# The transposed stream in the stream's own tiles, where the first norm sums; the last strip's token halves end apart; the last scaling fused

## The chip, the core and the metric

The kernel runs on one core of a Trainium2 chip. The metric is the device time of one execution in microseconds (us). The time of the kernel before is the median of three runs. Beside them one execution was profiled; its trace is what the numbers below come from.

## What is computed

A decoder trunk of two layers on 256 tokens of width 2048, all in float32. Shortened from the reference:

```python
def reference(x, p, positions, ...):
    for i in range(2):
        h = rms_norm(x, attn_norm_w[i])
        if i == 0:
            x = x + mixer_a(h, a_w_qkv[i], a_w_o[i])      # stick-breaking attention
        else:                                             # i == 1
            k_blocks, v_blocks = shared_kv_blocks(x, kv_norm_w, b_w_kv, positions)
            x = x + mixer_b(h, b_w_q[0], b_w_o[0], k_blocks, v_blocks, positions)
        x = x + conv_ffn(rms_norm(x, ffn_norm_w[i]), ...)
        gate = sigmoid(rms_norm(x, ple_norm_w[i]) @ ple_w_gate[i])
        x = x + gate * (p[i] @ ple_w_proj[i])
    return rms_norm(x, final_norm_w)

def rms_norm(x, w):
    return x * rsqrt(mean(x * x, axis=-1) + 1e-6) * w
```

The change touches the first rms_norm, in front of the first product with a_w_qkv, and the end of the program: the gate of layer 1, its product, and the last rms_norm.

## The kernel before

**Tiles.** A block is 128 of the 2048 model columns; there are 16. The stream x lives in SBUF as two tiles `x[0]`, `x[1]` of 128 tokens by 2048 columns. Products need the stream transposed, as blocks of 128 columns by 256 tokens; the host hands in such a copy, `xT`, for the first norm and product.

**Split products.** A float32 operand is split into a high part, rounded to the matmul's format, and the low rest. `weights` (lines 201 to 221) loads weights into `raw` over the SP queue (four buffers), copies the high part `whi` on ACT (ScalarE) and subtracts the low part `wlo` on DVE (VectorE); `whi` and `wlo` have four buffers of two blocks each. `split_x` (lines 128 to 138) does the same to a stream block after multiplying it by the norm's gain: `h` has its high half from ACT (L133) and its low half from DVE (L134). The norm's row factor 1/rms is not in h; it is applied to the product.

**Strips.** A product is done in strips of 512 output columns. `strip_t` (lines 237 to 250) makes four transposed outputs, one PSUM bank each, and takes the blocks in pairs: for one output of one pair a group of two matmuls with whi (512 wide) and two with wlo (256 wide). `strip_v` (lines 252 to 264) makes one output per token half, three matmuls of 512 columns per block. `steps` (lines 223 to 235) holds the last `tail` blocks back and goes through them output by output, so that the outputs end one after the other. Five banks, tag "acc", serve these products. The banks of a `strip_t` are emptied by `evac` (lines 266 to 273): ACT copies the correction (L268), DVE adds (L269) and multiplies by the row factor (L273).

**The first strip.** `strip_t(wqkv, 0, h, True, load_x)` (L595) loads its weights two blocks at a time, 512 KB, and calls `load_x` (lines 589 to 593) for every pair: a transfer of 256 KB into a ring tile `xT`, then `split_x`. Behind it `late_loads` (lines 109 to 117) loads constants and the 2 MB of x over ACT's queue, and the first `Norm` squares x strip by strip on ACT (L161), sums along the row, makes 1/rms by logarithm and exponential and one step of refinement (lines 167 to 177), and turns it into a row over all partitions by a matmul with a diagonal (lines 180 to 186).

**The end.** In `ple` of layer 1 the last strip (s = 3) runs the small product first, then the gate's; per token half come the sigmoid on ACT (L562), the product and the addition on DVE (L567, L568), the square (L161), and the multiplication by the last norm's gain (L571). Then the last norm, and lines 617 to 624: the eight pieces of 128x512 are scaled by 1/rms, the first token half on DVE (L621), the second on ACT (L623), and stored over SP's and ACT's queues (L624).

**What sets the order.** The program is written in one order, and a scheduler makes from it one queue of instructions per engine, which the engine runs in that order, waiting on semaphores. The weights' splits get priority (`tc.high_priority(offset=AHEAD)`), so they stand ahead of their place. A transfer waits in its queue until the buffer it writes is free, and the transfers behind it wait with it. In the queues before, two groups of the second strip stand in front of the end of the first one, and the first norm's matmul stands in its middle.

## Time and profile before

| what | value |
|---|---|
| time, median of 3 runs | 2397.92 us (2396.64 to 2398.55) |
| profiled execution | 2399.31 us |
| its span in the trace | 2397.5 us |
| busy: TensorE matmuls / weight loads | 2363.2 / 2003.5 us |
| busy: VectorE / ScalarE | 1561.1 / 1271.8 us |
| moved by DMA | 442.82 MB, 185 GB/s on average |
| chain of work that ended last | TensorE 97% of the span |

A busy figure is the sum over the whole span; what a stage is limited by is read from that stage. The span is 1.8 us shorter than the execution's time. In the rows, PE is TensorE, PEld its weight loads, SPq and ACTq the DMA queues of SP and ACT, and L220 is line 220 of the kernel before. A timeline's row can hold several instructions (x2); then the second number is the time from the first one's start to the last one's end. Matmuls are pipelined, so the rows of one engine overlap.

### The profile page before, as it was taken

To read this page: it belongs to the slowest core of one execution; us is meant where nothing else is said; L and a number is where in the kernel's file an instruction comes from. 1 tells how busy PE (TensorE), PEld (TensorE's weight loads), DVE (VectorE), ACT (ScalarE), POOL (GpSimd) and SP (SyncE) were. 2 spreads that over 40 slices of the span, in tenths; PEclk is the share of its full clock that TensorE was granted. 3 is DMA by queue.
4 is the path that set the end of the run, shared out by engine and by line. 5 is a ranking of instruction groups with operands and counts; after the bars stand their busy time and mean duration, and the time that the engine had idled before them with its cause. 6 is when DMAs were issued, how large, how long until landed. Compare 5 with 4: busy or idle time off the path is not lost.

```text
span 2397.5 us, 31193 instructions
## 1 busy us (share of the span) xinstructions
PE 2363.2 (99%) x12260; PEld 2003.5 (84%) x12260; DVE 1561.1 (65%) x2364; ACT 1271.8 (53%) x1829; POOL 0.2 (0%) x4
## 2 busy tenths in 40 slices
PE   6999999999999999999999999999999999999997
PEld 5888888888888888888888888888888888888886
DVE  5555555777864477775568875667776457876564
ACT  5555455655553355554565444556555345655454
POOL 0000000000000000000000000000000000000000
PEclk8999999999999999999999999999999999999999
DMA  6444445555555555555555444555555555555553
GB/s 261 168 169 173 176 158 192 182 193 194 181 190 194 193 191 194 188 184 191 186 185 190 174 163 153 181 189 186 191 194 190 194 192 184 189 193 189 183 200 114
DMA packets 64852, 442.82 MB, mean 185 GB/s; under 512 B 7328, under 2 KB 7488, under 8 KB 12736
## 3 DMA queue, kind: packets, MB, share of 16 engines
q1 hardware_dynamic: 62352, 435.19, 51.3%
q10 hardware_dynamic: 2352, 5.63, 0.6%
q8 instruction: 96, 1.57, 0.2%
q14 instruction: 52, 0.43, 0.0%
HBM read 438.69 MB, written 2.10 MB: 184 GB/s over the span
## 4 chain that ended last, share of the span: by engine, by line
PE 97%; ACT 1%; DMA 1%; DVE 1%; issue 0%; SPq 0%; ACTq 0%; DVEq 0%
PE acc L246 35%; PE acc L249 18%; PE accv L262 14%; PE accv L261 14%; PE accv L263 14%; PE two L197 1%; PE po L287 1%; DMA xT<-in_xT 1%; ACT whi L219 0%; DVE wlo L220 0%; DMA vec<-in_vec 0%; PE two L345 0%; PE po L288 0%; PE two L429 0%; PE two L359 0%
## 5 line engine op out<-in xcount | busy, mean ns | idle before, releaser
L220 DVE TENSOR_TENSOR wlo<-raw,whi 128x1024 fp32r<-128x1024 f32 (+1 forms) x825 | 1008.5, 1222 | 758.6 <-ACT whi L219 754.6
L219 ACT ACTIVATE whi<-raw 128x1024 fp32r<-128x1024 f32 (+1 forms) x825 | 872.9, 1058 | 921.2 <-PE accv L263 455.9
L246 PE MATMUL acc<-h,whi 128*128 128x512 f32 x3712 | 1174.8, 398 | 19.0 <-DVE h L134 18.8
L249 PEld LDWEIGHTS acc<-h,wlo 128*128 128x128 f32 x3712 | 698.8, 189 | 164.1 <-DVE wlo L220 1.1
L249 PE MATMUL acc<-h,wlo 128*128 128x256 f32 x3712 | 733.8, 279 | 0.7 <-DVE wlo L220 0.7
L246 PEld LDWEIGHTS acc<-h,whi 128*128 128x128 f32 x3712 | 570.1, 190 | 22.5 <-DVE h L134 20.1
L262 PE MATMUL accv<-wlo,g 128*128 128x512 f32 x704 | 274.6, 390 | 0.0
L263 PE MATMUL accv<-whi,g 128*128 128x512 f32 x704 | 274.5, 390 | 0.0
L261 PE MATMUL accv<-whi,g 128*128 128x512 f32 x704 | 274.1, 389 | 0.0
L261 PE MATMUL accv<-whi,h 128*128 128x512 f32 x480 | 188.5, 393 | 0.0
L262 PE MATMUL accv<-wlo,h 128*128 128x512 f32 x480 | 188.5, 393 | 0.0
L263 PE MATMUL accv<-whi,h 128*128 128x512 f32 x480 | 188.1, 392 | 0.0
L263 PEld LDWEIGHTS accv<-whi,g 128*128 128x128 f32 x704 | 132.5, 188 | 26.9
L261 PEld LDWEIGHTS accv<-whi,g 128*128 128x128 f32 x704 | 132.2, 188 | 27.2
L262 PEld LDWEIGHTS accv<-wlo,g 128*128 128x128 f32 x704 | 132.2, 188 | 27.1
L268 ACT ACTIVATE c<-acc 128x256 f32<-128x256 f32 x232 | 86.7, 374 | 35.8 <-PE acc L249 35.8
L263 PEld LDWEIGHTS accv<-whi,h 128*128 128x128 f32 x480 | 90.3, 188 | 17.8
L261 PEld LDWEIGHTS accv<-whi,h 128*128 128x128 f32 x480 | 90.2, 188 | 17.5
L262 PEld LDWEIGHTS accv<-wlo,h 128*128 128x128 f32 x480 | 90.2, 188 | 17.5
L269 DVE TENSOR_TENSOR c<-acc,c 128x256 f32<-128x256 f32 x232 | 91.8, 416 | 0.3 <-ACT c L268 0.3
L262 PE MATMUL accv<-wlo,o 128*128 128x512 f32 x224 | 88.2, 394 | 0.0
L263 PE MATMUL accv<-whi,o 128*128 128x512 f32 x224 | 88.2, 394 | 0.0
(149 smaller groups left out, 1394.4 us busy)
## 6 DMA issues: line engine op xcount, KB each, us to landing
raw<-in_wup SPq DMA_DIRECT2D x176, 1024.0 KB, 4.8
raw<-in_wdn SPq DMA_DIRECT2D x88, 1024.0 KB, 4.8
raw<-in_wqkv SPq DMA_DIRECT2D x44, 1024.0 KB, 4.8
raw<-in_wpg SPq DMA_DIRECT2D x32, 1024.0 KB, 4.8
raw<-in_wkv SPq DMA_DIRECT2D x24, 1024.0 KB, 4.8
raw<-in_wo_a SPq DMA_DIRECT2D x16, 1024.0 KB, 4.8
raw<-in_wq_b SPq DMA_DIRECT2D x12, 1024.0 KB, 4.7
raw<-in_wo_b SPq DMA_DIRECT2D x12, 1024.0 KB, 4.8
```

The lines of the kernel that those rows point to most:

```text
L197: nc.tensor.transpose(d[:, t * P : (t + 1) * P], x[t][:, c : c + P], idf)
L219: nc.scalar.activation(hi[:, c], r, AF.Copy)
L220: nc.vector.tensor_tensor(lo[:, c], r, f32(hi[:, c]), op=OP.subtract)
L246: nc.tensor.matmul(ps[o], hi[:, c], xs[k], start=k == 0, stop=False)
L249: nc.tensor.matmul(ps[o][:, S:], lo[:, c], xs[k][:, :S], start=False, stop=k == n - 1)
L261: nc.tensor.matmul(ps[t], xl, hi, start=k == 0, stop=False)
L262: nc.tensor.matmul(ps[t], xh, lo, start=False, stop=False)
L263: nc.tensor.matmul(ps[t], xh, hi, start=False, stop=k == n - 1)
L268: nc.scalar.activation(c, ps[:, S:], AF.Copy)
L269: nc.vector.tensor_tensor(c, ps[:, :S], c, op=OP.add)
L287: nc.tensor.matmul(po[:, :S], v[0][:, c], a0, start=True, stop=False)
```

## The change

- The transposed stream is loaded into the two stream tiles `x[0]`, `x[1]` themselves (eight blocks in each), not into ring tiles. The token-major x is loaded into the same tiles only after the first norm, behind the first strip.
- The first norm becomes `FirstNorm`: each transposed block is squared on ACT and added up on DVE, two blocks behind the load (LAG), and at the end a matmul with ones sums over the 128 columns of a block for all partitions at once, which gives the row factor; two one-column matmuls give it as columns. The steps to 1/rms then run on 128x258 elements, not on 128x2.
- `strip_v` takes `tail`; the last strip's gate holds six blocks instead of two.
- For the last strip the gain is not multiplied in before the norm, but together with the row factor in one instruction behind it.
- The last scalings go in the order of strips 0, 3, 1, 2; strip 3 on DVE (fused), the first half of strip 0 on DVE, the other five on ACT.
- `rstd` has one buffer instead of two, the steps to 1/rms stand in one function `rsqrt`, and the norms' small tiles are reused.

```diff
@@ -63,6 +63,7 @@
 
 
 RAW = 4
+LAG = 2
 NRING, NRAW, NWSP = 42, 4, 4
 AHEAD = 200
 KV_AT = (0, 6, 12, 16)
@@ -110,8 +111,6 @@
         nc.scalar.dma_start(c32, cst_d)
         nc.scalar.dma_start(cbf, csb_d)
         nc.scalar.dma_start(vec[:, KB:], vec_d[:, KB:])
-        for t in range(2):
-            nc.scalar.dma_start(x[t], x_d[t])
         nc.vector.tensor_copy(idf, IDB)
         nc.scalar.activation(NT, c32[:, C_NT : C_NT + P], AF.Copy)
         nc.scalar.activation(NONE, c32[:, C_NONE : C_NONE + P], AF.Copy)
@@ -144,17 +143,57 @@
     def strip_of(t, s):
         return x[t][:, s * 512 : (s + 1) * 512]
 
+    def load_table():
+
+        table = nc.scalar.preload_act_table_set("natural_log_exp_and_others")
+        tc.keep_in_program_order(table)
+        return table
+
+    def rsqrt(v, y, t, table):
+
+        nc.vector.tensor_scalar(v, v, 1.0 / D, EPS, op0=OP.mult, op1=OP.add)
+        with tc.issue_after(table.ins):
+            nc.scalar.activation(y, v, AF.Ln)
+            nc.scalar.activation(y, y, AF.Exp, scale=-0.5)
+        nc.vector.tensor_tensor(t, y, y, op=OP.mult)
+        nc.vector.scalar_tensor_tensor(t, t, -0.5, v, op0=OP.mult, op1=OP.mult)
+        nc.vector.scalar_tensor_tensor(v, t, 1.5, y, op0=OP.add, op1=OP.mult)
+
+    class FirstNorm:
+
+
+        def __init__(self):
+            self.s = tt("first", bufs=1)
+            self.n = 0
+            self.table = load_table()
+
+        def add(self, src):
+            if self.n == 0:
+                nc.scalar.activation(self.s, src, AF.Square)
+            else:
+                q = tt("sq", tag="t", bufs=6)
+                nc.scalar.activation(q, src, AF.Square)
+                nc.vector.tensor_tensor(self.s, self.s, q, op=OP.add)
+            self.n += 1
+
+        def done(self):
+            ps = bank("nrm")
+            nc.tensor.matmul(ps[:, :S], ONE, self.s, start=True, stop=False, skip_group_check=True)
+            for t in range(2):
+                c = slice(S + t, S + t + 1)
+                nc.tensor.matmul(
+                    ps[:, c], self.s[:, t * P : (t + 1) * P], ONE[:, :1], start=False, stop=t == 1, skip_group_check=True
+                )
+            r = tt("rstd1", (P, S + 2), bufs=1)
+            nc.vector.tensor_copy(r, ps[:, : S + 2])
+            rsqrt(r, *(tt("n", (P, 768), tag="w", bufs=2)[:, : S + 2] for _ in range(2)), self.table)
+            return r[:, :S], r[:, S:]
+
     class Norm:
 
 
         def __init__(self):
             self.s = tt("ssum", (P, 2, 4), bufs=2)
-            self.table = None
-
-        def load_table(self):
-
-            self.table = nc.scalar.preload_act_table_set("natural_log_exp_and_others")
-            tc.keep_in_program_order(self.table)
 
         def add(self, s, t):
             q = tt("sq", (P, 768), tag="e", bufs=1)[:, :512]
@@ -162,19 +201,9 @@
 
         def done(self, row=True):
 
-            small = lambda n: tt(n, (P, 2), bufs=2)
-            v = small("nv")
-            nc.vector.reduce_sum(v, self.s, axis=mybir.AxisListType.X)
-            nc.vector.tensor_scalar(v, v, 1.0 / D, EPS, op0=OP.mult, op1=OP.add)
-            y = small("ny")
-            with tc.issue_after(self.table.ins):
-                nc.scalar.activation(y, v, AF.Ln)
-                nc.scalar.activation(y, y, AF.Exp, scale=-0.5)
-            t = small("nt")
-            nc.vector.tensor_tensor(t, y, y, op=OP.mult)
-            nc.vector.scalar_tensor_tensor(t, t, -0.5, v, op0=OP.mult, op1=OP.mult)
-            rc = small("rcol")
-            nc.vector.scalar_tensor_tensor(rc, t, 1.5, y, op0=OP.add, op1=OP.mult)
+            rc = tt("rcol", (P, 2), bufs=2)
+            nc.vector.reduce_sum(rc, self.s, axis=mybir.AxisListType.X)
+            rsqrt(rc, *(tt("n", (P, 2), bufs=2) for _ in range(2)), self.table)
             if not row:
                 return None, rc
             dg = tt("diag", tag="t", bufs=6)
@@ -249,11 +278,11 @@
                 nc.tensor.matmul(ps[o][:, S:], lo[:, c], xs[k][:, :S], start=False, stop=k == n - 1)
         return ps
 
-    def strip_v(W, s, xs, base=0):
+    def strip_v(W, s, xs, base=0, tail=2):
 
         n = len(xs)
         ps = [None] * 2
-        for k, t, hi, lo in (g for group in steps(weights(W, s, n, base=base), n, 2) for g in group):
+        for k, t, hi, lo in (g for group in steps(weights(W, s, n, base=base), n, 2, tail) for g in group):
             if k == 0:
                 ps[t] = bank("accv", "acc")
             xh = xs[k][:, t * P : (t + 1) * P]
@@ -553,7 +582,7 @@
             end = gain_of is None and s == 3
             if end:
                 pr = strip_v(wpp[i], s, ps_)
-            gp = strip_v(wpg[i], s, xs)
+            gp = strip_v(wpg[i], s, xs, tail=6 if end else 2)
             if not end:
                 pr = strip_v(wpp[i], s, ps_)
             ts = []
@@ -562,12 +591,12 @@
                 nc.scalar.activation(g, gp[t], AF.Sigmoid, scale=rc[:, t : t + 1])
                 ts.append(g)
             if s == 3:
-                norm.load_table()
+                norm.table = load_table()
             for t, g in enumerate(ts):
                 nc.vector.tensor_tensor(g, pr[t], g, op=OP.mult)
                 nc.vector.tensor_tensor(strip_of(t, s), strip_of(t, s), g, op=OP.add)
                 norm.add(s, t)
-                if gain_of is None:
+                if gain_of is None and not end:
                     nc.vector.tensor_tensor(strip_of(t, s), strip_of(t, s), gf[s], op=OP.mult)
             if gain_of is not None:
                 two, bs = turn(s)
@@ -577,27 +606,32 @@
                     raw += [r[:, :S], r[:, S:]]
                     for q in range(2):
                         out += split_x(bs[o + q], 4 * s + o + q, [gain_of])
-        return out, raw
+        return out, raw, gf
 
 
     idf = cst.tile([P, P], F32, name="idf")
-    norm = Norm()
-    norm.load_table()
+    norm = FirstNorm()
     nc.scalar.dma_start(vec[:, :KB], vec_d[:, :KB])
     h = [None] * KB
 
+    xT = [x[j // 8][:, j % 8 * S : (j % 8 + 1) * S] for j in range(KB)]
+
     def load_x(k0):
-        t = rt("xT")
-        nc.sync.dma_start(t.rearrange("p (a b) -> p a b", a=2), xT_d[:, k0 : k0 + 2, :])
-        for q in range(2):
-            (h[k0 + q],) = split_x(t[:, q * S : (q + 1) * S], k0 + q, [G_ATTN])
+        t = x[k0 // 8].rearrange("p (a b) -> p a b", b=S)
+        nc.sync.dma_start(t[:, k0 % 8 : k0 % 8 + 2, :], xT_d[:, k0 : k0 + 2, :])
+        for j in (k0, k0 + 1):
+            (h[j],) = split_x(xT[j], j, [G_ATTN])
+        for j in range(k0 - LAG, k0 - LAG + 2):
+            if j >= 0:
+                norm.add(xT[j])
 
     first = strip_t(wqkv, 0, h, True, load_x)
     late_loads()
+    for j in range(KB - LAG, KB):
+        norm.add(xT[j])
+    rstd, rc = norm.done()
     for t in range(2):
-        for s in range(4):
-            norm.add(s, t)
-    rstd, rc = norm.done()
+        nc.scalar.dma_start(x[t], x_d[t])
     o = mixer_a(h, rstd, rc, first)
     for i in range(2):
         norm = Norm()
@@ -608,19 +642,21 @@
         _, rc = norm.done(row=False)
         norm = Norm()
         if i == 0:
-            hq, xT = ple(i, h, pb, rc, norm, G_ATTN + KB)
+            hq, xT, _ = ple(i, h, pb, rc, norm, G_ATTN + KB)
             rstd, rc = norm.done()
             o = mixer_b(hq, lambda js: [split_x(xT[j], j, [G_KV])[0] for j in js], rstd, rc)
         else:
-            ple(i, h, pb, rc, norm)
+            _, _, gf = ple(i, h, pb, rc, norm)
             _, rc = norm.done(row=False)
-    for s in range(4):
+    for i, s in enumerate((0, 3, 1, 2)):
         for t in range(2):
-            c = strip_of(t, s)
-            if t == 0:
-                nc.vector.tensor_scalar(c, c, rc[:, t : t + 1], None, op0=OP.mult)
+            c, r = strip_of(t, s), rc[:, t : t + 1]
+            if s == 3:
+                nc.vector.scalar_tensor_tensor(c, c, r, gf[s], op0=OP.mult, op1=OP.mult)
+            elif t == 0 and s == 0:
+                nc.vector.tensor_scalar(c, c, r, None, op0=OP.mult)
             else:
-                nc.scalar.activation(c, c, AF.Copy, scale=rc[:, t : t + 1])
+                nc.scalar.activation(c, c, AF.Copy, scale=r)
             (nc.sync, nc.scalar)[t].dma_start(out_d[t][:, s * 512 : (s + 1) * 512], c)
 
 
```

How it moves instructions. The first place is SP's queue at the start of the program. raw is a weight tile of the first strip, xT_ a ring tile of the transposed stream, x_74 and x_75 the stream's tiles; the waits name semaphores of transfers (DMAHW) and of VectorE. Before:

```order
L211 DMA raw_85<-in_wqkv 128x512 x2
L591 DMA xT_90<-in_xT 128x512
L211 DMA raw_122<-in_wqkv 128x1024
L211 DMA raw_152<-in_wqkv 128x1024
L591 DMA xT_126<-in_xT 128x512 [waits DMAHW1_49]
L211 DMA raw_182<-in_wqkv 128x1024 [waits DMAHW2_49]
L211 DMA raw_212<-in_wqkv 128x1024 [waits DMAHW4_49,DMAHW0_49,DVE_49]
L211 DMA raw_242<-in_wqkv 128x1024 [waits DMAHW5_49,DVE_49]
L211 DMA raw_272<-in_wqkv 128x1024 [waits DMAHW7_49,DMAHW6_49,DVE_49]
L591 DMA xT_156<-in_xT 128x512 [waits DMAHW0_49]
```

And now:

```order
L240 DMA raw_85<-in_wqkv 128x512 x2
L621 DMA x_74<-in_xT 128x512
L240 DMA raw_121<-in_wqkv 128x1024
L621 DMA x_74<-in_xT 128x512
L240 DMA raw_154<-in_wqkv 128x1024 [waits DMAHW0_49]
L621 DMA x_74<-in_xT 128x512 [waits DMAHW2_49]
L240 DMA raw_189<-in_wqkv 128x1024 [waits DMAHW3_49]
L621 DMA x_74<-in_xT 128x512 [waits DMAHW4_49]
L240 DMA raw_224<-in_wqkv 128x1024 [waits DMAHW5_49,DMAHW1_49,DVE_49]
L621 DMA x_75<-in_xT 128x512 [waits DMAHW6_49]
```

The transposed stream's transfers moved from behind the weights' to a place behind each one of them.

The second place is VectorE in the first strip. wlo is the low part of a pair of weight blocks, h the low half of one stream block, first_82 the sum of squares. Before, from the second pair on:

```order
L220 TENSOR_TENSOR wlo_125<-raw_122,whi_124 128x1024
L220 TENSOR_TENSOR wlo_155<-raw_152,whi_154 128x1024
L220 TENSOR_TENSOR wlo_185<-raw_182,whi_184 128x1024
L220 TENSOR_TENSOR wlo_215<-raw_212,whi_214 128x1024
L134 SCALAR_TENSOR_TENSOR h_128<-xT_126,vec,h_128 128x256
L134 SCALAR_TENSOR_TENSOR h_131<-xT_126,vec,h_131 128x256
L134 SCALAR_TENSOR_TENSOR h_158<-xT_156,vec,h_158 128x256
L134 SCALAR_TENSOR_TENSOR h_161<-xT_156,vec,h_161 128x256
L220 TENSOR_TENSOR wlo_245<-raw_242,whi_244 128x1024
```

And now, from the fourth pair on:

```order
L249 TENSOR_TENSOR wlo_192<-raw_189,whi_191 128x1024
L176 TENSOR_TENSOR first_82<-first_82,sq_165 128x256
L133 SCALAR_TENSOR_TENSOR h_194<-x_74,vec,h_194 128x256
L176 TENSOR_TENSOR first_82<-first_82,sq_168 128x256
L133 SCALAR_TENSOR_TENSOR h_197<-x_74,vec,h_197 128x256
L249 TENSOR_TENSOR wlo_227<-raw_224,whi_226 128x1024
L176 TENSOR_TENSOR first_82<-first_82,sq_200 128x256
L133 SCALAR_TENSOR_TENSOR h_229<-x_75,vec,h_229 128x256
L176 TENSOR_TENSOR first_82<-first_82,sq_203 128x256
L249 TENSOR_TENSOR wlo_262<-raw_259,whi_261 128x1024
```

Four wlo in a row stood ahead of the second pair's h; now each pair has one wlo, two h and two additions.

The third place is ACT at the end of the program, from the last strip's first sigmoid (pg) on. sq is a square, ny or n the row factor's steps, x_74 and x_75 the two token halves. Before:

```order
L562 ACTIVATE pg_20276<-accv_20144,rcol_19591 128x512
L562 ACTIVATE pg_20278<-accv_20151,rcol_19591 128x512
L156 ACT_TABLE_LOAD
L161 ACTIVATE sq_20283,ssum_19593<-x_74 128x512
L161 ACTIVATE sq_20288,ssum_19593<-x_75 128x512
L171 ACTIVATE ny_20294<-nv_20291 128x2
L172 ACTIVATE ny_20294<-ny_20294 128x2
L623 ACTIVATE x_75<-x_75,rcol_20300 128x512 x2
L624 DMA out<-x_75 128x512 x2
L623 ACTIVATE x_75<-x_75,rcol_20300 128x512 x2
```

And now:

```order
L591 ACTIVATE pg_20289<-accv_20157,rcol_19596 128x512
L200 ACTIVATE sq_20296,ssum_19606<-x_74 128x512
L591 ACTIVATE pg_20291<-accv_20164,rcol_19596 128x512
L148 ACT_TABLE_LOAD
L200 ACTIVATE sq_20300,ssum_19606<-x_75 128x512
L156 ACTIVATE n_20304<-rcol_20302 128x2
L157 ACTIVATE n_20304<-n_20304 128x2
L659 ACTIVATE x_75<-x_75,rcol_20302 128x512
L659 ACTIVATE x_74<-x_74,rcol_20302 128x512
L660 DMA out<-x_75 128x512 x2
L659 ACTIVATE x_75<-x_75,rcol_20302 128x512
L659 ACTIVATE x_74<-x_74,rcol_20302 128x512
```

The first half's square moved ahead of the second half's sigmoid and of the table load; behind the norm ACT scales five pieces, one of them of the first half.

## Rows read from the trace of the kernel before

**Rows 1.** Windows: us, busy us per engine (instructions), clock, DMA share, GB/s
```profile
0.00:60.00 60.00, 40.27 (x183) 33.04 (x184) 34.88 (x69) 31.33 (x58) 0.20 (x4) 0.89 0.69 261
60.00:2380.00 2320.00, 2319.39 (x12064) 1967.88 (x12063) 1519.77 (x2281) 1233.27 (x1759) 0.00 (x0) 1.00 0.52 183
```
**Rows 2.** Waits of the first 80 us: us in total, times, longest
```profile
PE acc L246 <- DVE h L134: 18.8, 5, 7.8
```
**Rows 3.** Timeline of the SP queue, first 40 us: start, duration, instruction
```profile
1.64 0.42 SPq L591 DMA_DIRECT2D xT<-in_xT  x1
...
38.49 0.90 SPq L591 DMA_DIRECT2D xT<-in_xT  x2
```
**Rows 4.** Timeline of TensorE, first 53 us (idle before, releaser)
```profile
7.79 3.78 PE L246 MATMUL acc<-h,whi 128*128 128x512 f32 x8 [7.79 <-DVE h L134]
11.37 1.25 PE L249 MATMUL acc<-h,wlo 128*128 128x256 f32 x8
...
19.00 1.06 PE L246 MATMUL acc<-h,whi 128*128 128x512 f32 x2
...
20.28 1.05 PE L246 MATMUL acc<-h,whi 128*128 128x512 f32 x2
...
35.80 0.59 PE L184 MATMUL nrm<-diag,c 128*128 128x256 f32 x2
...
38.53 0.50 PE L246 MATMUL acc<-h,whi 128*128 128x512 f32 x1 [1.21 <-DVE h L134]
...
51.02 0.39 PE L249 MATMUL acc<-h,wlo 128*128 128x256 f32 x2
...
51.71 0.40 PE L249 MATMUL acc<-h,wlo 128*128 128x256 f32 x2
```
**Rows 5.** Groups by line and shape: busy us, mean ns | idle before
```profile
L220 DVE TENSOR_TENSOR wlo<-raw,whi 128x1024 fp32r<-128x1024 f32 x823 | 1007.1, 1224 | 753.5 <-ACT whi L219 749.5
L219 ACT ACTIVATE whi<-raw 128x1024 fp32r<-128x1024 f32 x823 | 871.6, 1059 | 918.7 <-PE accv L263 455.9 <-PE acc L246 387.7 <-ACT c L268 24.1
...
L142 DVE TENSOR_TENSOR g<-val,g 128x256 fp32r<-128x256 f32 x88 | 36.8, 418 | 0.0
...
L133 ACT ACTIVATE h<-xT,vec 128x256 fp32r<-128x256 f32 x32 | 14.2, 496 | 6.6 <-DMA xT<-in_xT 6.6
L134 DVE SCALAR_TENSOR_TENSOR h<-xT,vec,h 128x256 fp32r<-128x256 f32 x32 | 14.0, 471 | 5.7 <-ACT h L133 5.7
```
**Rows 6.** Timeline of all engines, last strip and last norm
```profile
2373.80 1.23 DVE L220 TENSOR_TENSOR wlo<-raw,whi 128x1024 fp32r<-128x1024 f32 x1 [1.49 <-ACT whi L219]
...
2383.17 0.39 PE L263 MATMUL accv<-whi,h 128*128 128x512 f32 x1
...
2384.30 1.28 ACT L156 ACT_TABLE_LOAD   x1
...
2385.04 0.69 DVE L568 TENSOR_TENSOR x<-x,pg 128x512 f32<-128x512 f32 x1
...
2386.34 0.63 ACT L161 ACTIVATE sq<-x 128x512 f32<-128x512 f32 x1
2386.35 1.45 DVE L571 TENSOR_TENSOR x<-x,gfin 128x512 f32<-128x512 f32 x2 [0.62 <-ACT sq L161]
...
2387.71 0.15 DVE L167 TENSOR_REDUCE nv<-ssum 128x2 f32<-128x8 f32 x1
```
**Rows 7.** Timeline of the stores' issues on SP and on ACT's queue
```profile
2389.67 2.46 SPq L624 DMA_DIRECT2D out<-x  x4
...
2392.30 1.03 ACTq L624 DMA_DIRECT2D out<-x  x1
```
**Rows 8.** Windows: the stretch of the stores
```profile
2390.50:2396.00 5.50, 0.00 (x0) 0.00 (x0) 0.33 (x1) 1.33 (x2) 0.00 (x0) 0.50 1.01 377
```
**Rows 9.** Windows: TensorE's granted clock in the first strip
```profile
30.00:32.00 2.00, 1.30 (x3) 1.11 (x4) 1.09 (x4) 1.85 (x6) 0.00 (x0) 0.50 1.00 399
...
38.00:40.00 2.00, 1.47 (x9) 1.33 (x10) 1.97 (x8) 0.29 (x1) 0.00 (x0) 1.00 0.38 70
```

More of the change, by code (lines that the diff above doesn't have):

```diff
@@ L184, in done @@
             nc.tensor.matmul(ps[:, :S], ONE, dg, start=True, stop=True)
-            r = tt("rstd", bufs=2)
+            r = tt("rstd", bufs=1)
             nc.scalar.activation(r, ps[:, :S], AF.Copy)
@@ L564, in ple @@
             if s == 3:
-                norm.load_table()
+                norm.table = load_table()
             for t, g in enumerate(ts):
@@ L579, in ple @@
                         out += split_x(bs[o + q], 4 * s + o + q, [gain_of])
-        return out, raw
+        return out, raw, gf
     idf = cst.tile([P, P], F32, name="idf")
-    norm = Norm()
-    norm.load_table()
+    norm = FirstNorm()
     nc.scalar.dma_start(vec[:, :KB], vec_d[:, :KB])
     h = [None] * KB
+    xT = [x[j // 8][:, j % 8 * S : (j % 8 + 1) * S] for j in range(KB)]
     def load_x(k0):
-        t = rt("xT")
-        nc.sync.dma_start(t.rearrange("p (a b) -> p a b", a=2), xT_d[:, k0 : k0 + 2, :])
-        for q in range(2):
-            (h[k0 + q],) = split_x(t[:, q * S : (q + 1) * S], k0 + q, [G_ATTN])
+        t = x[k0 // 8].rearrange("p (a b) -> p a b", b=S)
[5 more added lines that the diff above has]
+                norm.add(xT[j])
     first = strip_t(wqkv, 0, h, True, load_x)
     late_loads()
+    for j in range(KB - LAG, KB):
+        norm.add(xT[j])
+    rstd, rc = norm.done()
     for t in range(2):
-        for s in range(4):
-            norm.add(s, t)
-    rstd, rc = norm.done()
+        nc.scalar.dma_start(x[t], x_d[t])
     o = mixer_a(h, rstd, rc, first)
```

## The prediction

> **What bounds the kernel now.** I read the windows first, then the waits and the timeline of the two ends. Between 60 and 2380 us TensorE is busy for all but 0.6 us of 2320, at full clock, so nothing there can be won by an edit that leaves the matmuls as they are; in the first 60 us it is busy for only 40.27 [rows 1]. Nearly all of that hole is one kind of wait: TensorE stood 18.8 us, in five stretches, for the low halves of h, which VectorE makes from the transposed stream (7.8 of them before the first matmul) [rows 2]. So the stream arrives late, not the weights. The SP queue says why: its first xT transfer is issued at 1.64 us, the last two at 38.49 [rows 3], because weight transfers that wait for buffers stand ahead of them. Of the span's end I read each engine's timeline: the last matmul ends at 2383.56 [rows 6], and 13.9 us of the span follow in which TensorE does nothing.
>
> The middle is the same in the changed kernel but for the tiny operations of the norms, so the sum has two terms, the first strip and the end.
>
> **The first strip: what the change does.** The eight xT transfers now go alternately with the eight weight transfers of the strip, the 2 MB of x on ACT's queue go behind the strip, and the eight squares of 128x512 with their sums become sixteen squares of 128x256 on ACT and fifteen additions on VectorE, two of each per pair of k-blocks.
>
> Where TensorE stood before: the strip's last group (two 512-wide, two 256-wide matmuls) ends at 51.71 + 0.40 = 52.11, and the pitch of a group is 51.71 - 51.02 = 0.69 [rows 4]. In front of it lay two groups of the second strip and the first norm's matmul. Without the two groups the mark is 52.11 - 1.38 = 50.73.
>
> Where it stands after: the first pair of blocks does not change. Its matmuls start at 7.79 and end at 11.37 + 1.25 = 12.62 [rows 4]; the transfers in front of it are the same. Then seven pairs. What paces them:
> - TensorE: four groups, 4 x 0.69 = 2.76 us at the full clock.
> - VectorE: one wlo, two low halves of h, two additions. 1.22 + 2 x 0.471 + 2 x 0.418 = 3.00 us [rows 5]; the addition is priced by the 128x256 subtraction of g.
> - ACT: one whi, two h, two squares. No 128x256 square is in the trace; at the 0.496 of h, which reads a per-partition scale as well and so is the upper bound, it is 1.06 + 4 x 0.496 = 3.04 us [rows 5]. From below the pair can't go under VectorE's figure, so the square's price hardly matters.
> - DMA: 768 KB per pair. At the 377 GB/s that the engines reach while they are full [rows 8] that is 2.04 us. A weight transfer's buffer is free once the wlo four pairs earlier is done, so it is issued some 12 us ahead of its use. I cost it at nothing; if the engines gave only the 261 GB/s of the first 60 us before [rows 1], a pair would take 2.94 and still be covered.
>
> VectorE is the slowest by a little, so I take 3.00 a pair: 12.62 + 7 x 3.00 = 33.62. From below the bound is TensorE's own 2.76: 31.9. From above I add the 753.5 / 823 = 0.92 us that VectorE waits beside an average wlo [rows 5], 3.92 a pair: 40.1.
>
> Behind the strip stand the norm's matmul, 0.59 [rows 4], and two new one-column matmuls, which no row shows; they cost from nothing to 0.59 together, I take 0.1. That makes 34.3 against 50.73.
>
> One wait is added there. The whi that uses the strip's last buffer now stands on ACT ahead of the logarithm and of the copies that empty the strip's banks, and the second strip has one free bank, so TensorE does four groups of its first output and then needs an emptied bank. The chain from the strip's end: whi 1.06, wlo 1.22, then the 258-wide copy, the scaling, the logarithm, the bank's copy and its addition, five at 0.42 to 0.50 [rows 5] = 2.3, in all 4.6. TensorE's cover is 0.7 + 4 x 0.69 = 3.5. So up to 1.1 us of waiting; nothing at best, since VectorE may take the scaling later. I take 0.9. What is queued behind it on ACT are the other three bank copies, and TensorE waits for those too, each some 0.5 apart, which the groups in between cover.
>
> First strip: 50.73 - 34.3 - 0.9 = 15.5 us. The bounds give 18.2 (2.76 a pair, no wait: 50.73 - 31.9 - 0.6) and 8.8 (3.92 a pair, 1.1 of wait).
>
> The late load of x (2 MB) shares the DMA engines with the second strip's weights; those engines are busy for 0.52 of the time in the steady stretch [rows 1] and x is read hundreds of us later, so it costs nothing.
>
> **The end.** Before, ACT loads the table at 2384.30 for 1.28 us, then squares the first half, and starts the second half's square only at 2386.34, though the second half was complete when its addition ended, 2385.04 + 0.69 = 2385.73. Then VectorE multiplies both halves by the gain (two instructions, 1.45 us from 2386.35), and the sums are reduced only at 2387.71 [rows 6].
>
> After: the held part of the last strip is six blocks instead of two, so the first half's matmuls end 18 matmuls instead of six ahead of the end, some 4 us, which hides its sigmoid, product, addition and square. The second half's square then starts at 2385.73 + 0.04, 0.57 us earlier. And the gain's two products are gone from in front of the reduction: the second of them could start only when the second square had ended, at 2386.35 + 1.45 - 0.69 = 2387.11, so the reduction can start there and not at 2387.71, 0.60 us earlier [rows 6]. Together 1.17 us. From there to the scale factors the same seven small operations run. The weights of the last pair must be split earlier; VectorE has the last at 2373.80 + 1.23 = 2375.03 [rows 6], 8.5 us before the last matmul's end, and they are needed 24 matmuls, some 5.5 us, before it, so nothing waits.
>
> The eight stores come next. Before, they keep the DMA engines at 1.01 of capacity from 2390.50 to 2396.00 [rows 8], so their end follows from their start, and the first is issued at 2389.67 [rows 7], behind one 128x512 scaling on VectorE as after the change. After, VectorE does that scaling and two fused ones, which I price at the 0.69 of a 128x512 product [rows 6]; ACT does five scalings instead of four, beside four issues. ACT's second issue waits for VectorE's third scaling (1.4 us behind the first issue); then come two scalings of some 0.7, an issue of 0.4, a scaling and the last issue, 3.9 us behind the first, against 2392.30 - 2389.67 = 2.6 before [rows 7]. A store holds the engines for 5.5 / 8 = 0.69 us, so the eighth is due 7 x 0.69 = 4.8 us behind the start of the first, and can flow 3.9 us behind it. The engines don't run dry, and the whole 1.2 us is kept. The bounds are 1.4 and 0, the latter if the end follows the last issue instead (1.3 later, relative to the first).
>
> **Sum.** 15.5 + 1.2 = 16.7 us off the profiled execution's 2399.31 (its span 2397.5 and 1.8 around it) is 2382.6. That execution is 1.4 above the median of the runs, 2397.92, so the median after is 2397.92 - 16.7 = 2381.2. The bounds together: 2397.92 - 19.6 = 2378.3 and 2397.92 - 8.8 = 2389.1.
>
> **The rivals.**
> 1. The clock. In the first 40 us the granted clock falls to 0.50, the 1.2 GHz level [rows 9], behind one of TensorE's long waits for h, and a group then takes 20.28 - 19.00 = 1.28 us [rows 4], that is 5.12 a pair. If waits at every pair kept it at the lower level for half of the seven pairs, the strip would end at 33.6 + 3.5 x 2.1 = 41.0 and the total be 2388.6; for all of them at 48.5, and the total 2396.1. Against it: behind the wait of 1.21 us that ends at 38.53 [rows 4] the window shows 1.00 [rows 9], and the waits that I expect are below 0.5 us.
> The Trainium skill, "TensorE: Matmul & The Clock Gate", section "HAM oscillation — how this bites in real kernels", describes a loop that falls back to the lower clock at each k-step since each ends in a wait for data; by that rule this strip, whose every pair now waits a little for VectorE, would come out at 2396.1. The rows agree with it for the long waits and not for the one of 1.21 us.
> 2. Slower than before. ACT and VectorE now feed each other in order: ACT's square waits for a buffer that an addition on VectorE frees, the addition for a square on ACT. If the two queues ran in turn instead of side by side, a pair would take 3.04 + 3.00 = 6.04 us, the strip end at 54.9, and TensorE be 54.9 + 0.7 + 0.9 - 50.73 = 5.8 us late; less the 1.2 of the end that is 2402.5. It decides from 5.4 us a pair. For it: VectorE's idle time is already put down to whi almost alone [rows 5]. Against it: six buffers of squares, four of whi and wlo, and whi ahead of the squares of the pair before.
> 3. The end gives nothing back, since its length follows from ACT's last issue and not from the first: 2382.4. For it: ACT's chain there is longer by a scaling. Against it: the engines are full for the whole 5.5 us.
>
> **Chances.** The forecast 0.80, rival 1 0.10, rival 2 0.03, rival 3 0.07. The bounds above are the range, 2378.3 to 2389.1; they hold rival 3 and the milder half of rival 1. A change of 0.2%, 4.8 us, is about what a measurement of this kernel can tell from none; only rival 1's full case falls inside it: faster 0.95, the same 0.03, slower 0.02.
>
> **What would show it.** Right: TensorE's waits for h in the first strip shrink from 18.8 us to some 10, 7.8 of them before its first matmul; the strip's last group ends near 34; the granted clock stays at 1.00 behind the first pair; the reduction of the last norm follows the second half's square at once, about 3 us behind the last matmul; stores fill 5.5 us. Wrong: pairs at over 4 us, a window at 0.50 between 13 and 40 us, or a wait of over 2 us for an emptied bank at the second strip's start.

## The result, and the profile after

| what | before | changed |
|---|---|---|
| median | 2398.55 us (2396.64 to 2399.46, 5 runs) | 2386.14 us (2383.66 to 2387.31, 5 runs) |
| span of the profiled execution | 2397.5 | 2384.3 |
| last matmul's end | 2383.56 | 2371.51 |
| from there to the span's end | 13.94 | 12.79 |

The ratio of changed to before is 0.9948, 95% interval 0.9933 to 0.9962. By the medians 12.4 us were gained, by the two profiled spans 13.2; the prediction had 16.7. The time lies in its range, 4.9 us above the forecast.

The windows of [rows 1], in the changed kernel (us, busy us per engine, clock, DMA share, GB/s):

```profile
0.00:60.00 60.00, 48.82 (x266) 42.02 (x267) 47.38 (x91) 37.05 (x66) 0.20 (x4) 1.00 0.82 313
60.00:2380.00 2320.00, 2310.94 (x11999) 1958.78 (x11998) 1518.28 (x2284) 1234.84 (x1764) 0.00 (x0) 1.00 0.52 182
```

TensorE gained 8.5 us of work in the first 60 us, and the clock there reads 1.00 instead of 0.89. The middle is as full as it was (in the second row 8.5 of the 9.1 idle us are the end, which now begins at 2371.51). What is left of TensorE's waits, against [rows 2] (total, times, longest):

```profile
PE acc L275 <- DVE h L133: 7.9, 1, 7.9
PE two L374 <- DVE qk L300: 2.7, 1, 2.7
PE acc L275 <- DVE c L298: 0.5, 1, 0.5
```

All waits for h but the first are gone. The third line is the wait for an emptied bank that was forecast as 0.9; the second, the largest, was not forecast at all. TensorE's timeline has the pace of the strip, the norm and that wait; compare [rows 4]:

```profile
7.93 3.78 PE L275 MATMUL acc<-h,whi 128*128 128x512 f32 x8 [7.93 <-DVE h L133]
...
31.87 0.40 PE L278 MATMUL acc<-h,wlo 128*128 128x256 f32 x2
32.10 0.60 PE L181 MATMUL nrm<-first,c 128*128 128x256 f32 x2
32.53 0.50 PE L184 MATMUL nrm<-c,first 128*128 128x1 f32 x4
32.89 0.71 PE L275 MATMUL acc<-h,whi 128*128 128x512 f32 x2
...
36.44 0.70 PE L275 MATMUL acc<-h,whi 128*128 128x512 f32 x2 [0.51 <-DVE c L298]
...
59.63 1.22 PE L374 MATMUL two<-qk,qk 128*128 128x256 f32 x2 [2.75 <-DVE qk L300]
...
62.64 0.62 PE L290 MATMUL accv<-whi,h 128*128 128x512 f32 x1
```

The strip ends at 31.87 + 0.40 = 32.27, so a pair took (32.27 - 12.74) / 7 = 2.79 us: TensorE's own four groups of 0.69, with nothing in between. At 59.63 the first head group's scores need qk, the second strip's emptied banks, and wait 2.75 us. Before, the same matmul ran at 73.72 without a wait. The clock behind it:

```profile
58.00:60.00 2.00, 0.36 (x1) 0.37 (x2) 2.00 (x6) 0.33 (x1) 0.00 (x0) 0.88 0.96 406
60.00:62.00 2.00, 2.00 (x7) 1.64 (x7) 2.00 (x5) 0.06 (x1) 0.00 (x0) 0.50 0.00 0
62.00:64.00 2.00, 2.00 (x10) 1.69 (x9) 1.87 (x6) 0.94 (x2) 0.00 (x0) 0.76 0.83 205
```

It fell to 0.50, the 1.2 GHz level, and was back at 1.00 from 64 us on. Measured at the same matmul in both kernels, the lead over before is 73.72 - (59.63 - 2.75) = 16.8 us in front of the wait, 14.1 behind it, 12.5 at the first accv matmul behind the scores (75.16 before, 62.64 now), and 12.05 at the last matmul. The wait took 2.75, the low clock some 1.6; the 0.5 that goes later I can't assign.

Why qk is late stands on VectorE (start, us, instruction, idle before and releaser):

```profile
38.00 1.10 DVE L302 SCALAR_TENSOR_TENSOR qk<-c,rstd 128x256 f32<-128x256 f32 x3
42.39 0.28 DVE L327 CAST rot<-posi 32x256 f32<-32x256 int32 x1 [3.29 <-DMA posi<-in_pos]
...
58.51 0.73 DVE L298 TENSOR_TENSOR c<-acc,c 128x256 f32<-128x256 f32 x2
59.17 0.74 DVE L300 TENSOR_TENSOR qk<-c,rstd 128x256 f32<-128x256 f32 x2
```

and on ACT's queue:

```profile
26.03 0.33 ACTq L634 DMA_DIRECT2D x<-in_x  x1
32.20 0.34 ACTq L634 DMA_DIRECT2D x<-in_x  x1
35.61 0.34 ACTq L325 DMA_DIRECT2D posi<-in_pos  x1
```

The rotary angles begin with a cast of the positions, a transfer of 32 KB. It is now issued behind the 2 MB of x on ACT's queue, and lands 6.8 us later; before, x was issued at 8.00 and 14.87, long done, and the same transfer, issued at 36.44, took 1.8. VectorE stands 3.29 us at the cast, and the emptying of the second strip is behind it in its queue. The late x also keeps the DMA engines full around the positions' transfer; the last two columns are their share and GB/s, first before, then changed:

```profile
34.00:40.00 6.00, 4.79 (x23) 3.79 (x22) 3.39 (x9) 2.52 (x5) 0.00 (x0) 0.87 0.37 111
34.00:40.00 6.00, 5.50 (x32) 4.66 (x31) 4.27 (x12) 2.74 (x7) 0.00 (x0) 1.00 1.00 414
```

The Trainium skill, "DMA: Bandwidth & Descriptors", section "Queues, rings and completion order", says that on each engine the descriptors of one queue are consumed in the order of its ring; by that a small transfer starts only behind the descriptors of a large one in front of it. The changed kernel agrees: 249 of x's 256 packets on ACT's queue start before the first packet of the positions, at 39.57 us. But this is not shown to be what makes the landing slow. With nothing of x issued in front of it, and the engines just as full (share 1.01 from 22 to 28 us), the same transfer took 5.3 us in e5 below.

The end, against [rows 6, 7, 8]:

```profile
2371.12 0.39 PE L292 MATMUL accv<-whi,h 128*128 128x512 f32 x1
...
2373.78 0.63 ACT L200 ACTIVATE sq<-x 128x512 f32<-128x512 f32 x1 [0.24 <-DVE x L597]
...
2374.53 0.16 DVE L205 TENSOR_REDUCE rcol<-ssum 128x2 f32<-128x8 f32 x1 [0.85 <-ACT sq L200]
...
2376.51 3.42 SPq L660 DMA_DIRECT2D out<-x  x4
2376.74 1.44 ACTq L660 DMA_DIRECT2D out<-x  x2
...
2380.21 0.34 ACTq L660 DMA_DIRECT2D out<-x  x1
```

The reduction starts 3.02 us behind the last matmul's end (4.15 before), and the last issue 3.7 behind the first (2.6 before; 3.9 was worked out). The span's end came 1.15 us closer to the last matmul.

### The profile page after: what moved, and what is told of

Read it like the earlier page. It is cut to its first block, busy times and chain, and to the rows that moved or that the text cites. A ratio compares the mean times of both kernels' runs of the same rounds, so it can differ in the third digit from the quotient of the medians.

```text
span 2384.3 us, 31227 instructions
## 1 busy us (share of the span) xinstructions
PE 2359.8 (99%) x12264; PEld 2000.8 (84%) x12264; DVE 1565.7 (66%) x2374; ACT 1272.1 (53%) x1829; POOL 0.2 (0%) x4
## 4 chain that ended last, share of the span: by engine, by line
PE 97%; DVE 1%; ACT 1%; DMA 0%; issue 0%; SPq 0%; DVEq 0%; ACTq 0%
PE acc L275 36%; PE acc L278 18%; PE accv L290 14%; PE accv L291 14%; PE accv L292 14%; PE two L226 1%; DVE wlo L249 1%; PE po L316 1%; PE two L374 0%; ACT whi L248 0%; PE po L317 0%; PE two L458 0%; PE two L388 0%; DMA x<-in_xT 0%; PE two L375 0%
```

## The experiments

The theory: the positions queue behind x, so they come late, VectorE stalls, TensorE waits and its clock falls. The rival: not the transfer but the rotary chain's some thirty small operations, which formerly lay in the first strip's slack, fill VectorE in the second strip. A second question is which part of the change made the first strip faster. A profile's first matmul starts anywhere from 7.4 to 8.6 us, so marks are compared to about half a microsecond. Each run's ratio is to the kernel before on the same chip, whose medians there were 2397.89 us (e1 to e4), 2398.23 (e5 to e8) and 2398.96 (e9 to e11).

**Positions ahead of x** (e1):

```diff
+    posi = cst.tile([ROT, S], I32, name="posi")
     def late_loads():
+        nc.scalar.dma_start(posi, ...)        # in_pos, from rotary_angles
```

> The 32 KB of positions are issued on ACT's queue ahead of the 2 MB of x instead of behind them; the rest is the changed kernel. Theory (the queue): VectorE's cast of the positions no longer waits (3.3 us in the changed kernel), the second strip's last bank is emptied some 3 us earlier, TensorE's wait of 2.75 us for qk near 59 us and the 1.2 GHz stretch behind it (60 to 62 us, about 1.6 us) are gone: 2386.1 - 4.4 = about 2381.7. Rival (the work): it is the rotary chain's own thirty small operations, some 12 us on VectorE in the second strip, which delay the emptying; they stay, so TensorE still waits over 1.5 us there and the time is 2385 to 2386.

Measured 2385.44 us (2383.88 to 2385.95), ratio 0.9947 [0.9934, 0.9959]. The time is the rival's, but not by the rival's wait:

```profile
PE acc L277 <- DVE c L300: 2.2, 1, 2.2
```

No wait for qk is left; a wait for an emptied bank of 2.2 us, with the clock at 0.50 from 42 to 44 us, has taken its place. The scheduler had put the chain's first dozen operations in front of the first strip's emptying on VectorE:

```profile
37.28 0.40 DVE L340 SCALAR_TENSOR_TENSOR rot<-rnl,rot 32x256 f32<-32x256 f32 x1
...
39.06 0.41 DVE L340 SCALAR_TENSOR_TENSOR rot<-rnl,rot 32x256 f32<-32x256 f32 x1
39.40 0.41 DVE L300 TENSOR_TENSOR c<-acc,c 128x256 f32<-128x256 f32 x1
```

So this run moved two things and decides nothing alone.

**x behind the positions** (e2):

```diff
-    for t in range(2):
-        nc.scalar.dma_start(x[t], x_d[t])      # behind the first norm
             if g == 1:
                 rotary_angles()
+                for t in range(2):
+                    nc.scalar.dma_start(x[t], x_d[t])
```

> The two 1 MB transfers of x are issued behind the positions, in the place in the program where the rotary angles are made. Theory (the queue): as with the positions moved ahead, no wait of the cast, no wait of TensorE for qk, about 2381.7. Rival (the work): 2385 to 2386, TensorE still waiting over 1.5 us for qk.

Measured 2383.15 us (2382.98 to 2383.77), ratio 0.9939 [0.9926, 0.9951]. No wait for qk (the matmul runs at 58.72), no window below 1.00. The sign is the theory's; the size is 3.0 of the 4.4. One thing expected did not come: the cast, now at 32.88, still waits 1.6 us, since the positions, issued at 26.77 with x only behind them, took 6.1 us to land. TensorE waits 0.7 us for the norm's sum, whose addition stands behind the cast.

**Positions ahead, rotary chain held back** (e3), with e1's edit and

```diff
-        nc.vector.tensor_copy(r, pi)
+        with tc.issue_after(last):             # the second head group's last split
+            nc.vector.tensor_copy(r, pi)
```

> The positions are issued ahead of x, and the rotary chain's operations are held back until the second head group's products, some 150 us later, so VectorE does not have them in the second strip at all. Theory (the queue): nothing more than with the positions ahead alone, about 2381.7, the same within 0.5. Rival (the work): this one alone gives the 4.4 us, about 2381.7 where the positions ahead alone give 2385 to 2386. A mixture would show as TensorE's wait for qk being partly left in the former and gone here.

Measured 2382.80 us (2382.76 to 2383.03), ratio 0.9937 [0.9924, 0.9951]. No wait for qk, no window below 1.00. Taken with e1's time alone, this is what the rival expected; the next run tells the two apart.

**Positions ahead, the changed kernel's order** (e5), the decisive one: e1, but the cast is held behind the first norm's last step, where it was.

```diff
+        with tc.issue_after(first_norm.last):
+            nc.vector.tensor_copy(r, pi)
```

> The positions are issued ahead of x, but the rotary chain is kept behind the first norm's last step on VectorE, so that ACT and VectorE have the changed kernel's order to within a place or two and only the wait for the positions can go. Theory (the queue): the cast does not wait (3.3 us before), VectorE reaches the second strip's banks 3 us earlier, TensorE's wait for qk (2.75 us) and the 1.2 GHz stretch behind it go; the wait for an emptied bank near 36 us stays at 0.5 to 1 us, and the time is 2381.5 to 2383. Rival (the work): the chain's thirty operations are still there, TensorE still waits over 1.5 us for qk and the time is 2385 to 2386.

Measured 2382.78 us (2382.65 to 2383.53), ratio 0.9935 [0.9923, 0.9948]. TensorE's waits, and VectorE's cast and second emptying:

```profile
PE acc L277 <- DVE h L135: 8.5, 2, 8.0
PE acc L277 <- DVE c L300: 1.0, 1, 1.0
```

```profile
39.33 0.28 DVE L329 CAST rot<-posi 32x256 f32<-32x256 int32 x1
...
56.94 0.74 DVE L300 TENSOR_TENSOR c<-acc,c 128x256 f32<-128x256 f32 x2
57.61 0.74 DVE L302 TENSOR_TENSOR qk<-c,rstd 128x256 f32<-128x256 f32 x2
```

The positions, issued at 22.91, land 5.3 us later, long before the cast. The cast does not wait, qk is ready 1.6 us earlier, and the scores' matmul runs at 58.20 without a wait, the clock at 1.00. That is 15.5 us ahead of before, the prediction's figure for the first strip, but by chance: this run has waits of its own, 0.5 us for h and 1.0 for a bank. In this run and in the changed kernel the same 21 operations of the rotary chain stand on VectorE in front of the second strip's emptying. With e3, where they are gone and the time is the same, the rival falls: the work costs nothing there, the wait for its input did. Only in front of the bank additions (e1) does the work cost.

What these runs do not separate is why the input was late. Issued 9 to 13 us earlier (e1, e2, e3, e5), the positions are in time, or nearly so, although they still take 4.9 to 6.1 us with nothing of x in front. So standing behind x makes only some 0.7 to 1.9 of the changed kernel's 6.8 us, by this comparison; the rest goes with full engines. These are full of x too: with x issued only at 158.93 us (e10 below) their share from 34 to 38 us is 0.48. In each reading it is x in front of the positions that makes them late.

**2 MB more in the first strip** (e4): eight transfers of 256 KB, on ACT's queue, in `load_x` of the second and third pair.

```diff
+        if k0 in (2, 4):
+            for s in range(4):
+                nc.scalar.dma_start(rt("spare"), x_d[k0 // 2 - 1][:, s * 512 : (s + 1) * 512])
```

> The changed kernel, with 2 MB (eight transfers of 256 KB into spare buffers, read by nobody) added on ACT's queue during the first strip, where the kernel before loaded x. Prediction's step (DMA covered, 2.04 us of 2.79 a pair): the first strip's last group still ends at 32.3 us, at most 0.5 later, so the order of the transfers alone gave the first strip's gain. Rival: the DMA engines are the bound in this stretch (their share is 1.0 from 4 to 40 us), 2 MB at some 380 GB/s take 5.5 us, the strip ends near 37.5 and TensorE waits for h or whi several us more; then taking x out of the strip was the larger part of the gain.

One run, 2391.16 us. TensorE waits for h 13.7 us instead of 7.9, the clock is at 0.50 from 22 to 26 us, the norm's matmul at 41.30 instead of 32.10. The strip's last group ends at 41.45, where the prediction's step had 32.8 at most and the rival 37.5. But ACT's order had moved as well:

```profile
17.25 1.06 ACT L248 ACTIVATE whi<-raw 128x1024 fp32r<-128x1024 f32 x1 [1.95 <-DMA raw<-in_wqkv]
...
19.62 1.06 ACT L248 ACTIVATE whi<-raw 128x1024 fp32r<-128x1024 f32 x1 [1.31 <-DVE wlo L249]
...
20.58 0.89 ACT L132 ACTIVATE h<-x,vec 128x256 fp32r<-128x256 f32 x2
```

Two whi of later pairs, each waiting for its transfer or buffer, stand in front of the h that TensorE wants; in the changed kernel h is never behind two of them. So the loss belongs to the load and the order together, and I don't read a price of the load from it.

**The order of the transfers alone** (e8): the kernel before, with its old norm and with x loaded in the first strip, but every transfer of the strip kept in program order.

```diff
-        nc.sync.dma_start(t.rearrange(...), xT_d[:, k0 : k0 + 2, :])
+        tc.keep_in_program_order(nc.sync.dma_start(t.rearrange(...), xT_d[:, k0 : k0 + 2, :]))
                 # the same for the first two strips' weights
```

> The kernel before with only the order of the transfers changed: each pair's piece of the transposed stream behind that pair's weights, as in the changed kernel; x is still loaded during the first strip, and the first norm is the old one. Theory as the prediction had it (the order of the transfers is what made the stream late, the DMA engines cover their load): the strip's last group ends near 33 us and the time is about 2385. Theory from the run with 2 MB added: the DMA engines are full in the strip, x's 2 MB push the stream and the weights out by 5 to 6 us and the clock falls behind the wait; the last group ends near 41 us and the time is 2388 to 2392.

Measured 2384.98 us (2384.67 to 2385.22), ratio 0.9944 [0.9930, 0.9958]. This is the main gain. It is not told apart from the whole change by the two ratios' intervals. But against the start of the change alone (e7 below), on the same chip and with the same end, it is 2.9 us faster, and the two runs' ranges lie apart. TensorE's timeline, its two waits for h behind the first, and the norm:

```profile
16.77 0.97 PE L248 MATMUL acc<-h,whi 128*128 128x512 f32 x3 [0.77 <-DVE h L134]
...
23.90 0.96 PE L248 MATMUL acc<-h,whi 128*128 128x512 f32 x3 [1.25 <-DVE h L134]
...
35.63 0.40 PE L251 MATMUL acc<-h,wlo 128*128 128x256 f32 x2
35.86 0.60 PE L184 MATMUL nrm<-diag,c 128*128 128x256 f32 x2
```

The strip's last group ends at 36.03, 3.8 later than in the changed kernel and 3 later than the first theory said: two waits for h make 2.0 us of that, shorter gaps the rest. How much of it is x in the strip and how much the old norm, no run separates. It is far from the 41 of the other theory. But x is through before the positions are issued (they land in 3.7 us), so nothing waits at 59.67, where the scores' matmul stands: level with the changed kernel's 59.63. The new norm and the late x bought 3.8 us, gave them back at the positions, and then lost more to the low clock, which e8 does not have.

**The end alone, and the start alone** (e6, e7): the two halves of the diff, each without the other.

> The kernel before with the end's edits alone (six blocks held in the last strip, the gain fused into the last scaling, the order of the last scalings). Prediction's step: the reduction follows the last matmul's end by 3.0 us instead of 4.15, span end minus last matmul's end is 12.8 instead of 13.9, and the time is 1.2 below the kernel before. Rival (the end's length follows from ACT's last issue): the reduction is earlier, but the stores end no earlier, 13.9 us.

> The changed kernel with the end of the kernel before. If the two parts add up: 1.2 us above the changed kernel, 2387.3; the first 70 us as in the changed kernel, with the wait for qk of some 2.7 us. If the six held blocks disturb the last strip or help it beyond the tail, the difference is another: 0 or over 2 us.

The end alone: 2397.74 us (2396.37 to 2398.78, 10 runs), ratio 0.9997 [0.9988, 1.0007], 0.5 below before and not told from no change by its interval, which holds the expected 1.2 as well. Its trace has the edit's effect: the reduction at 2385.86 is 3.02 us behind the last matmul's end at 2382.84, and the span's end 12.86. The start alone: 2387.84 us (2386.92 to 2388.66), ratio 0.9956 [0.9942, 0.9969], 1.7 above the changed kernel, with 13.98 us behind the last matmul and the wait for qk at 2.4. The tails of 12.79 and 12.86 with the edit, 13.94 and 13.98 without, show the 1.1 us; the two parts add up within the runs' scatter.

**A version that beats both** (e9, e10): e9 is e5 with the weights' priority for the first norm and the first strip's emptying; e10 has x issued some 130 us later as well (158.93 instead of 27.25). Beside them, on the same chip, the changed kernel once more (e11).

```diff
+    with tc.high_priority(offset=AHEAD):
         rstd, rc = norm.done()
...
+                        with tc.high_priority(offset=AHEAD if g == 0 and which == 0 else 0):
                             evac(...)
```

> As the run with the positions early and the order kept, and the first strip's banks and the first norm get the weights' priority, so that three bank additions stand ahead of the next weight pair on VectorE. Theory (the queue, and what is left is the bank wait): TensorE's wait for an emptied bank near 37 us shrinks from 0.98 to under 0.3, the rest stays; 2382.0 to 2382.8, 0.7 below that run at most. Rival (VectorE's work is conserved): the weights' low parts come later in turn, TensorE waits for wlo or qk instead and the time is 2382.8 or more.

> As the run before in this list, and x's two transfers are issued only behind the first head groups, near 150 us. Theory (x's 2 MB behind the first strip cost nothing by themselves, only through the positions queued behind them): the same as without, 2382.0 to 2382.8. Rival (they also slow the second strip's weights): another 0.5 to 1.5 us less, 2381 to 2382.

> The changed kernel unaltered, beside the two others on one chip: 2386.1 by its first runs, with TensorE's wait for qk of 2.5 to 3 us and the granted clock at 0.50 behind it.

e9: 2382.71 us (2382.44 to 2383.12), ratio 0.9933 [0.9919, 0.9947]. e10: 2381.94 us (2381.67 to 2382.40), ratio 0.9930 [0.9918, 0.9943], the fastest kernel of this study. e11: 2386.48 us (2386.23 to 2387.74), ratio 0.9950 [0.9938, 0.9963], with the wait for qk at 2.4. In e9 the bank wait is gone, but the norm's matmul waits 0.5 for the sum, and the time is e5's. In e10 TensorE waits for nothing behind its first matmul:

```profile
PE acc L277 <- DVE h L135: 7.6, 1, 7.6
```

That e10 is 0.8 below e9 is shown by the runs, and it is the figure of that run's rival (x slows the second strip's weights). But why is not shown: its first matmul starts 0.9 us earlier in the profiled executions, before the edit acts, and VectorE's order moved with x.

## Why the prediction was right in its direction and 4.9 us too low

**The step that failed** is the sentence "The late load of x (2 MB) ... costs nothing". Its first reason, that the DMA engines have room, took their 0.52 from the steady stretch; where x goes, from 26 to 40 us, their share is 1.01. Its second, that x is read much later, looked at x and not at what is issued behind it on ACT's queue: the positions, wanted at 39.1 us and landed at 42.4. That cost 2.75 us of waiting and some 1.6 of low clock in the trace. Without it (e5) the time is 2382.8, 3.4 less than the changed kernel's and 1.6 above the forecast.

**The first strip's pace**, 3.00 a pair, was sized 0.21 too high: 2.79. I added mean durations of VectorE's instructions, and these overlap. In the changed kernel's strip:

```profile
16.80 1.23 DVE L249 TENSOR_TENSOR wlo<-raw,whi 128x1024 fp32r<-128x1024 f32 x1
17.94 0.42 DVE L176 TENSOR_TENSOR first<-first,sq 128x256 f32<-128x256 f32 x1
18.28 0.48 DVE L133 SCALAR_TENSOR_TENSOR h<-x,vec,h 128x256 fp32r<-128x256 f32 x1
18.67 0.42 DVE L176 TENSOR_TENSOR first<-first,sq 128x256 f32<-128x256 f32 x1
19.17 1.23 DVE L249 TENSOR_TENSOR wlo<-raw,whi 128x1024 fp32r<-128x1024 f32 x1
```

An addition 0.42 long is followed after 0.34, a wlo 1.23 long after 1.14. One wlo, two h and two additions take 1.14 + 2 x 0.39 + 2 x 0.34 = 2.6 us, less than TensorE's 2.76, which is then the pace: the prediction's lower bound. The square on ACT took 0.40, not 0.496. The DMA step counts a KB as 1000 bytes; with 1024 its 2.04 and 2.94 us a pair are 2.09 and 3.01, and TensorE waited for no transfer of the strip behind its first matmul.

**The bank wait**, taken as 0.9, was 0.51; the two one-column matmuls, taken as 0.1, moved the next group by 32.89 - 32.53 = 0.36. Together these errors put the lead in front of the qk wait at 16.8 instead of 15.5: they were in the kernel's favour and hid part of what the positions cost.

**The end** was right term by term: 1.13 us at the reduction (1.17 forecast), 1.15 at the span's end (1.2).

**Rival 1, the clock**, did not come at the pairs: they ran back to back, every window from 8 to 58 us at 1.00. The prediction looked for a window at 0.50 between 13 and 40 us; it came at 60. Over the runs, the waits of 0.98 (e5) and 1.25 us (e8) were followed by no row below 1.00, those of 2.25 (e1), 2.75 (changed) and 4.23 (e4) by rows at 0.50. The rule of the Trainium skill that the prediction weighed ("TensorE: Matmul & The Clock Gate", "HAM oscillation — how this bites in real kernels") describes a loop that waits at each step for longer than it computes; the prediction carried it over to waits below 0.5 us, which the page does not state. This strip had no wait for h after its first, so it does not test that reading.

**Rival 2** (ACT and VectorE in turn) is excluded by the same rows, **rival 3** (the end gives nothing) by the tails of e6 and e7.

The reason for the gain was right, that the stream's transfers stood behind the weights': e8 alone takes 13.2 us off. The rest of the diff's start, the new norm in x's tiles, is worth the difference of e8 and e5 at the scores' matmul, 59.67 - 58.20 = 1.5 us, once the positions are early; as the change has it, it loses 2.9 us (e7 against e8).

## What to carry to other kernels

When a transfer is moved, look at what is issued behind it on the same queue and who reads that first: a small transfer that is wanted early goes ahead of a large one that is read late. Take the DMA engines' share from the stretch where the transfer will run, not from the average of another. A first instruction that waits for data stalls everything behind it on its engine, so the work that was free in a stretch with slack has to be placed again when the slack is taken away. To price an engine's queue, take start-to-start times from the timeline, not the sum of the durations.

## What the runs showed of the hardware

- VectorE's and ACT's instructions start 0.08 to 0.1 us before the recorded end of the one in front (VectorE in the rows above; on ACT two squares of 0.41 us start at 25.90 and 26.21), so sums of durations are too long by that much per instruction.
- In the changed kernel the DMA engines' share is 1.02 from 12 to 40 us. A transfer of 256 KB in the first strip took 6.8 us to land (median of eight), a weight piece of 512 KB 6.2 (median of seven), and still TensorE waited for none of them behind its first matmul.
- The 32 KB of the positions took 1.8 us to land with the engines' share at 0.37 (before, 34 to 40 us), 4.9 to 6.1 at 1.0 with nothing of x in front (e1, e2, e3, e5), and 6.4 to 6.8 at 1.0 behind x (changed, e7, e11).
